# Narrow and wide matmuls take turns on TensorE, gelu as one ScalarE function, zero matmuls and own load tiles at the start, the last token tile in column halves

## The chip, the cores and the metric

The kernel runs on one core of a Trainium2 chip. The metric is the device time of one execution in microseconds (us), as the median of several runs; less is better. The core's engines work side by side, each through its own list of instructions in a fixed order: TensorE (PE, matmuls; PEld is its weight load), VectorE (DVE), ScalarE (ACT), GpSimd (POOL) and SyncE (SP, which here issues nearly all DMA transfers). An instruction that waits holds up everything behind it on its engine.

## The reference, cut to what matters

The program is a decoder trunk of two layers on 512 tokens of width 1024. Every sub-layer is followed by x <- LayerNorm(alpha * x + sublayer(x)).

```python
# layer 0: gated DeltaNet (4 heads, chunks of 64 tokens, a recurrence over chunks)
#          and dilated sliding-window attention (8 heads) from one projection
proj = h @ w_in
dn_qkv, dn_z, dn_b, dn_a, sw_q, sw_k, sw_v = split(proj)
mix = concat([gated_deltanet(...), dilated_attention(...)]) @ w_out
# layer 1: S5, a diagonal complex state space, then gelu and a GLU
y = scan(a_bar, b_bar * u) projected back + d_skip * u
hid = jax.nn.gelu(y)                       # the tanh form
mix = (hid @ w_o) * jax.nn.sigmoid(hid @ w_g)
# both layers, after the mixer
h = post_norm(h, mix)
h = post_norm(h, memory_cross_attention(h, mem, ...))   # 256 memory tokens
h = post_norm(h, (silu(h @ wg) * (h @ wu)) @ wd)         # hidden width 2816
```

## The kernel before, in words

**Products.** A weight block is loaded as fp32 into a tile of the tag `raw` (two buffers), then split: ScalarE copies it rounded to the matmul type fp32r into `hi`, VectorE subtracts, raw - hi, into `lo` (four buffers each). Activations are split in the same way. `mm3` then makes three matmuls of each product, hi·hi, hi·lo and lo·hi. Such a matmul mostly has 512 moving columns (256 in places); these are called wide here. Narrow are the transposes (128x128, against `ident`) and the plain fp32 matmuls of the recurrence and of the attention, most of them 128x128 too. A plain fp32 128x128 matmul that is no transpose stands in the trace as two passes, so the page counts 8220 matmuls where the program has 7618.

**Order.** All work is recorded first, as operations with a priority, and nothing is issued while it is recorded. `Order.order` (line 282 on) then walks through a planned time: whenever an engine is free it takes, from a heap of operations whose inputs are ready in the plan, the one of the best priority whose tiles have a buffer, and books a cost from `Order.cost` (a transpose 0.11 us, a wide matmul of 512 columns 0.217 us, a plain fp32 128x128 matmul 0.217 us in the planner's table). The result is one fixed order for each engine, which `issue` (lines 430 to 439) writes out; hence nearly every row of the trace has line L439, or L437 where several small matmuls go together, and is told apart by the names of its tiles. What the planner believes about a time is not what the chip does: it decides only the order.

**Stages.** Layer 0 begins with `mixer0`: the x tiles and the first weight block of `hyb_w_in` (columns 512 to 768) are loaded at once with a bias of -1000 (lines 615 to 620), through the two `raw` buffers; small constants follow, then the other blocks. A block of 16 small columns of the weights (`t<-in_hyb_w_in_dram`) feeds the gates of the DeltaNet. A solve on VectorE, a chain of narrow matmuls and then a recurrence over chunks follow; wide matmuls of the projections are put between them as far as there are any. Two large constants, `big<-in_ident_dram` (the start value X of the solve) and `big<-in_attmask_dram` (the attention mask), are loaded on SP among the first loads. In layer 1, `s5` goes through eight blocks; each ends in a tile of 128x512 results in PSUM (`yp`), to which gelu is applied by four operations, then four transposes and a split. The GLU, cross-attention and the FFN follow; the FFN's last product (`gemm_tok`, sink `residual_sinks`, `norm_half`) goes token tile by token tile (four of 128 tokens), and the last one ends with VectorE's statistics, the normalisation and the store of the output.

Of the kernel before, what the change touches and what calls it, by code (L numbers as in the profile page):

```python
# [16 lines left out]
P = 128  # L17
# [15 lines left out]
TAIL = 8  # L33
TRIES = 40
FILL = 1
PRE = 1
GATE = 5
STEPS = (4, 2)
LATER = 100
# [65 lines left out]
class Order:  # L105
# [173 lines left out]
    def scratch(self, ap):  # L279
        self.hist.setdefault(ap.tensor.name, ([], []))  # L280


    def order(self, seq, prio):
# [37 lines left out]
        dma_free = 0.0  # L321
        slow = 3.4
        out = []
        for op in ops:
# [3 lines left out]
        while len(out) < n:  # L328
# [5 lines left out]
            for e in self.eng:  # L334
                if busy[e] > now + 1e-9:
                    nxt.append(busy[e])
                    continue
                skipped, got = [], None
                tries = 0
                while heaps[e]:  # L340
# [120 lines left out]
class Trunk:  # L461
# [103 lines left out]

    def gemm_tok_steps(self, w, k0, nk, c0, act, ntt, sink, tail=0):


        pss = [self.bank() for _ in range(ntt)]
        held = []  # L570
        for done in range(0, nk, 2):
            g = min(2, nk - done)
            hi, lo = self.weights(w, k0 + done, g, c0, 512)
            held += [(done + k, hi[:, k], lo[:, k]) for k in range(g)]
            if done + g <= nk - tail:
                self._tok_mms(held, range(ntt), pss, act, nk)
                held = []
                yield
        for tt in range(ntt):
            self._tok_mms(held, [tt], pss, act, nk)  # L580
            sink(tt, pss[tt])
            yield
# [17 lines left out]
    def mixer0(self, fill):  # L600
# [14 lines left out]
        self.o.bias = -1000  # L615
        for kh in range(2):
            view = w_in[kh * 512:kh * 512 + 512, 512:768].rearrange("(k p) c -> p k c", p=P)
            self.early[w_in.tensor.name, kh * 4, 512] = self._load(view, 4, 256, STEPS[kh], lambda s: [
                load_x(kh * 4 + k) for k in range(s * 4 // STEPS[kh], (s + 1) * 4 // STEPS[kh])])
        self.o.bias = 0  # L620
# [221 lines left out]
        def z_sink(tt, ps):  # L842
# [229 lines left out]
    def residual_sinks(self, half, alpha, eps, g, b, last, after):  # L1072

        V, G = self.o.V, self.o.G

        def sink(tt, ps):
            z = self.h[tt][:, half * 512:(half + 1) * 512]
            V.scalar_tensor_tensor(z, z, alpha, ps, op0=OP.mult, op1=OP.add)
            if last:
                self.norm_half(tt, half, eps, g, b, after)  # L1080
        return sink

    def norm_half(self, tt, half, eps, g, b, after):
        V, G = self.o.V, self.o.G
        if half == 0:
            self.stats[tt] = self.tiny(12)
        st = self.stats[tt]
        V.bn_stats(st[:, half * 6:half * 6 + 6], self.h[tt][:, half * 512:(half + 1) * 512])
        if half == 0:
            return  # L1090
        mv = self.tiny(3)
        V.bn_aggr(mv[:, 0:2], st.rearrange("p (n c) -> p n c", n=2))
        V.tensor_scalar(mv[:, 2:3], mv[:, 1:2], eps, None, op0=OP.add)
# [123 lines left out]
    def ffn(self, layer, after, fill=iter(())):  # L1217
# [5 lines left out]
        for part, (b0, b1) in enumerate(FFN_PARTS):  # L1223
# [30 lines left out]
            for half in range(2):  # L1254
                rs = self.residual_sinks(half, 2 * ALPHA if part == 0 else 1.0, 4 * LN_EPS, g, b, last, after)
                self.gemm_tok(wd, b0 * 2, nm, half * 512, htok, NT, rs, tail=TAIL)

# [239 lines left out]
    def s5(self, fill):  # L1497
# [4 lines left out]
        for b in range(8):  # L1502
# [39 lines left out]
            for q in range(4):  # L1542
# [23 lines left out]
    def glu_gate(self, gtok, half):  # L1566
        self.gate = {}

        def sink(tt, ps):
            self.gate[tt] = self.t2()  # L1570
            self.o.A.activation(self.gate[tt], ps, AF.Tanh, scale=0.25)
        return self.gemm_tok_steps(self.a["s5_glu_wg"][0], 0, KT, half * 512, gtok, NT, sink, tail=0 if half == 0 else TAIL)

    def glu(self, gtok):
# [9 lines left out]
        for half in range(2):  # L1584
            def osink(tt, ps):
# [3 lines left out]
                r3 = lambda x: x.rearrange("p (q c) -> p q c", c=32)  # L1589
                V.scalar_tensor_tensor(r3(z), hpv[half][:, tt], 4 * ALPHA, r3(t), op0=OP.mult, op1=OP.add)  # L1590
                self.norm_half(tt, half, 16 * LN_EPS, g, b, after)

# [69 lines left out]
    def setup(self):  # L1662
        nc = self.nc
        self.stats, self.hp, self.early = {}, None, {}
        self.ident = self.const([P, P], name="ident")
# [7 lines left out]
        self.halfpi = self.const([P, 1], name="halfpi")  # L1673
        self.o.V.memset(self.halfpi, math.pi / 2)


# [38 lines left out]
```

## Time and profile before

| | |
|---|---|
| median of 3 runs | 1544.35 us (1540.59 to 1544.91) |
| the profiled execution | 1543.56 us, span 1541.8 us, granted clock 0.995 |
| TensorE busy | 1508.7 us, 98% of the span |
| VectorE, ScalarE, GpSimd busy | 984.9, 552.5, 57.0 us |
| DMA | 184.01 MB, mean 119 GB/s |

The span runs from the first to the last recorded event of the profiled execution; 1.8 us of its time lie outside it. Busy times are sums over the engine's instructions. PE's rows show a duration that includes the pipe (a wide matmul of 0.39 us begins 0.23 us after the one before it), so distances between starts say more than durations.

### The profile page before, as it was taken

Reading aid. Unit: us, or ns where it says so; the run is one execution under the profiler, and the core shown is the slowest. Engines: PE = TensorE matmul, PEld = TensorE weight load, DVE = VectorE, ACT = ScalarE, POOL = GpSimd, SP = SyncE. Lnnn points to the kernel's source line nnn. Section 1 sums busy time; section 2 is a strip of 40 time slices with the busy share of each in tenths; the row PEclk is TensorE's granted clock in tenths of the full one; section 3 lists DMA queues with packets and bytes.
Section 4 is the critical chain, followed back from the end, with each engine's and each line's share of the span. In section 5 each row is a group of like instructions: output and inputs, shape, how many; then the busy total and the mean of one; then the engine's idle time right before and its main releaser. Section 6 shows DMA issues by size and latency. Waiting matters only on the chain.

```text
span 1541.8 us, 21120 instructions
## 1 busy us (share of the span) xinstructions
PE 1508.7 (98%) x8220; PEld 1268.3 (82%) x8220; DVE 984.9 (64%) x1880; ACT 552.5 (36%) x1008; POOL 57.0 (4%) x97
## 2 busy tenths in 40 slices
PE   7999899999999999999999899999999999999998
PEld 5888788689889887888888898888889888888886
DVE  6986576697557888626845899647557444234436
ACT  5533346544523354324341333323423222122311
POOL 1100000010100000010000000000000000000000
PEclk9999999999999999999999999999999999999999
DMA  6424134235223355445562652333212333233322
GB/s 201 115 57 123 47 119 137 64 98 163 62 76 116 110 192 176 150 165 174 186 220 76 245 191 86 128 110 121 65 57 82 109 99 102 85 110 96 96 69 96
DMA packets 125396, 184.01 MB, mean 119 GB/s; under 512 B 14128, under 2 KB 84656, under 8 KB 121200
## 3 DMA queue, kind: packets, MB, share of 16 engines
q1 hardware_dynamic: 125296, 182.66, 37.6%
q8 instruction: 65, 1.06, 0.3%
q14 instruction: 35, 0.29, 0.1%
HBM read 162.45 MB, written 20.19 MB: 118 GB/s over the span
## 4 chain that ended last, share of the span: by engine, by line
PE 88%; DVE 7%; DMA 2%; ACT 1%; issue 1%; SPq 0%; POOL 0%; DVEq 0%; ACTq 0%; POOLq 0%
PE ps L439 86%; DVE t L439 4%; DVE big L439 2%; PE ps L437 2%; DVE lo L439 1%; DMA raw<-in_hyb_w_in_dram 1%; DVE tiny L439 0%; DMA big<-s5m 0%; ACT big L439 0%; DMA raw<-in_xo_w_dram 0%; ACT hi L439 0%; ACT t L439 0%; DMA posi<-in_pos_t_dram 0%; SPq L439 0%; ACT L439 0%
## 5 line engine op out<-in xcount | busy, mean ns | idle before, releaser
L439 PE MATMUL ps<-big,hi 128*128 128x512 f32 (+1 forms) x2368 | 649.5, 360 | 6.1 <-ACT hi L439 4.5
L439 PE MATMUL ps<-hi,big 128*128 128x512 f32 x1728 | 548.2, 394 | 0.7 <-ACT big L439 0.4
L439 PEld LDWEIGHTS ps<-big,hi 128*128 128x128 f32 x2368 | 420.7, 190 | 72.4 <-ACT hi L439 4.7
L439 ACT ACTIVATE hi<-raw 128x1024 fp32r<-128x1024 f32 (+2 forms) x252 | 263.5, 1046 | 513.7 <-PE ps L439 355.7
L439 DVE TENSOR_TENSOR lo<-raw,hi 128x1024 fp32r<-128x1024 f32 (+2 forms) x252 | 303.4, 1205 | 224.8 <-ACT hi L439 221.4
L439 PE MATMUL ps<-big,lo 128*128 128x512 f32 (+1 forms) x1184 | 423.7, 359 | 2.5 <-DVE lo L439 2.5
L439 PEld LDWEIGHTS ps<-hi,big 128*128 128x128 f32 x1728 | 322.6, 188 | 66.4 <-DVE big L439 0.9
L439 PE MATMUL ps<-lo,big 128*128 128x512 f32 x864 | 338.3, 393 | 1.0 <-DVE lo L439 1.0
L439 PEld LDWEIGHTS ps<-big,lo 128*128 128x128 f32 x1184 | 224.6, 190 | 34.5 <-DVE lo L439 2.9
L439 PEld LDWEIGHTS ps<-lo,big 128*128 128x128 f32 x864 | 162.4, 188 | 35.5 <-DVE lo L439 2.2
L439 ACT ACTIVATE big<-ps 128x256 fp32r<-128x256 f32 (+2 forms) x188 | 89.4, 508 | 211.1 <-PE ps L439 202.0
L439 ACT ACTIVATE t<-ps 128x512 f32<-128x512 f32 (+6 forms) x147 | 68.8, 485 | 147.7 <-PE ps L439 139.0
L439 DVE TENSOR_TENSOR big<-ps,big 128x256 fp32r<-128x256 f32 (+1 forms) x152 | 77.6, 541 | 56.9 <-ACT big L439 54.7
L439 DVE SCALAR_TENSOR_TENSOR big<-big,ps 128x512 f32<-128x512 f32 x56 | 38.4, 685 | 86.7 <-PE ps L439 86.7
L439 DVE SCALAR_TENSOR_TENSOR t<-t,ps 128x512 f32<-128x512 f32 x72 | 49.0, 682 | 68.5 <-ACT t L439 49.8
L439 ACT ACTIVATE big<-t 32x128 f32<-32x128 f32 (+2 forms) x148 | 64.9, 455 | 24.3 <-DVE t L439 19.9
L439 DVE SCALAR_TENSOR_TENSOR big<-big,tiny,t 128x512 f32<-128x512 f32 x96 | 66.6, 745 | 0.0
L439 PE MATMUL ps<-ident,t 128*128 128x128 f32 x344 | 62.7, 275 | 3.4 <-ACT t L439 1.8
L439 POOL TENSOR_TENSOR tiny<-tiny,mhalf 128x1 f32<-128x1 f32 (+1 forms) x28 | 23.1, 825 | 962.3 <-DVE tiny L439 953.6
L439 PEld LDWEIGHTS ps<-ident,t 128*128 128x128 f32 x344 | 42.5, 140 | 15.6 <-ACT t L439 5.1
L439 PE MATMUL ps<-big,big 128*128 128x256 f32 (+2 forms) x328 | 54.9, 314 | 0.0
L439 PEld LDWEIGHTS ps<-big,big 128*128 128x128 f32 x328 | 47.8, 190 | 5.0
(145 smaller groups left out, 929.4 us busy)
## 6 DMA issues: line engine op xcount, KB each, us to landing
raw<-in_ffn_wg_dram SPq DMA_DIRECT2D x44, 512.0 KB, 3.8
raw<-in_ffn_wu_dram SPq DMA_DIRECT2D x44, 512.0 KB, 3.6
raw<-in_ffn_wd_dram SPq DMA_DIRECT2D x44, 512.0 KB, 4.1
s5m<-big SPq DMA_DIRECT2D x16, 1024.0 KB, 4.2
big<-s5m SPq DMA_DIRECT2D x16, 1024.0 KB, 6.3
raw<-in_hyb_w_in_dram SPq DMA_DIRECT2D x26, 512.0 KB, 3.8
raw<-in_xk_w_dram SPq DMA_DIRECT2D x16, 512.0 KB, 3.6
raw<-in_xv_w_dram SPq DMA_DIRECT2D x16, 512.0 KB, 4.1
```

The source lines that it names most:

```text
L437: op.inst = getattr(self.eng[e], f)(*a, **k)
L439: op.inst = getattr(self.eng[e], fn)(*args, **kw)
```

## The change

It has six parts. (1) `order` knows two kinds of TensorE operation. After a narrow one it looks, up to 200 entries deep (`WIDE`), for a wide one whose priority is at most 100 (`REACH`) behind the best narrow one, and takes it; and it books 0.08 us less for a narrow operation right after a wide one. (2) gelu is one ScalarE function, `Gelu_apprx_tanh`, in place of Square, a multiply-add on VectorE, Tanh and another; factors of 2 in the GLU are adapted. (3) `setup` puts 14 fp32 matmuls on a tile of zeros ahead of all else. (4) The first weight block goes to a tile of its own instead of the two `raw` buffers, and the second block (columns 768 to 1024) is loaded right behind it. (5) The loads of X and of the attention mask are made to wait for `egl`, a result of the gates, by a one-column copy into their tile. (6) In the second half of the last FFN product the last token tile is computed and normalised in column halves of 256 (60 matmuls of 256 columns in place of 30 of 512), with its statistics in quarters.

```diff
+WARM = 14
+WIDE = 200
+REACH = 100
...
+    def kind(op):
+        _, fn, args, kw, _ = op.alts[0]
+        if fn == "transpose":
+            return "narrow"
+        if fn == "matmul":
+            return "wide" if args[1].dtype == F32R and _size(op.outs[0]) >= 256 else "narrow"
+        return fn
...
+                    if ok and e == "pe" and after == "narrow" and (self.kind(op) != "wide" or narrow is not None and prio[op.i] > prio[narrow.i] + REACH):
+                        narrow = narrow or op
+                        ok = False
...
-                    if tries > TRIES:
+                    if tries > (TRIES if narrow is None else WIDE):
                         break
...
+                got = got or narrow
...
                     if e == "pe":
+                        kind = self.kind(op)
+                        if kind == "narrow" and after == "wide":
+                            cost -= 0.08
+                        after = kind
...
-    def _load(self, view, n, w, steps=1, between=None):
-        raw = self.o.tile(self.wp, [P, 1024], F32, self.nm("raw"), "raw", 2)
+    def _load(self, view, n, w, steps=1, between=None, raw=None):
+        raw = self.o.tile(self.wp, [P, 1024], F32, self.nm("raw"), "raw", 2) if raw is None else raw
...
+            if fine and tt == ntt - 1:
+                for u in range(2):
+                    split_mms(held, [u])
+                    sink(tt, own[u][:, :256], u)
...
+        own = self.big(F32)
+        for cb_ in range(2):
+            for kh in range(2):
+                c0 = 512 + cb_ * 256
...
+                self.early[w_in.tensor.name, kh * 4, c0] = self._load(view, 4, 256, STEPS[kh], lambda s: [
+                    load_x(kh * 4 + k) for k in range(s * 4 // STEPS[kh], (s + 1) * 4 // STEPS[kh])],
+                    own[:, kh * 1024:(kh + 1) * 1024]) if cb_ == 0 else self._load(view, 4, 256)
...
+        V.tensor_copy(X[:, 0, 0:1], egl[:64, 0:1])
         self.o.SP.dma_start(X, a["ident"][0:32, 0:32].partition_broadcast(64))
...
+        V.tensor_copy(attm[:, 0:1], egl[:, 0:1])
         self.o.SP.dma_start(attm, a["attmask"])
...
-            g1, g2 = self.t2(), self.t2()
-            A.activation(g1, yp, AF.Square)
-            V.scalar_tensor_tensor(g1, g1, 1.0 / 0.044715, yp, op0=OP.add, op1=OP.mult)
-            A.activation(g1, g1, AF.Tanh, scale=GELU_C * 0.044715)
-            V.scalar_tensor_tensor(g2, g1, 1.0, yp, op0=OP.add, op1=OP.mult)
+            g2 = self.t2()
+            A.activation(g2, yp, AF.Gelu_apprx_tanh)
...
+        self.o.bias = -3000
+        w, ps = self.t2(), self.bank()
+        self.o.V.memset(w[:, :P], 0.0)
+        for _ in range(WARM):
+            self.o.T.matmul(ps[:, :P], w[:, :P], w[:, :P], start=True, stop=True)
+        self.o.bias = 0
```

Over the whole program a narrow matmul stands directly behind a wide one 241 times before and 449 times after; the wide ones in front of the DeltaNet's chain of narrow matmuls (the one that starts with the transposes `ps<-ident,t` after the solve) number 500 before and 514 after, those inside it, up to the end of the recurrence's narrow run, 44 before and 30 after. ScalarE has 7 table loads after, 5 before. Three places show it.

On TensorE near the start, where the gates' small product (`masks,t`) and the first transposes of x's projections (`ident_72,big`, four to a bank) stand among the wide matmuls of the second weight block (`hi`, `lo`), the order before is:

```order
L439 MATMUL ps_114<-masks,t_39_113 128x8 x4
L439 MATMUL ps_156<-big_77,lo_160 128x512
L439 MATMUL ps_150<-ident_72,big_140 128x128 x4
L439 MATMUL ps_157<-big_77,hi_159 128x512 x2
L439 MATMUL ps_157<-big_77,lo_160 128x512
L439 MATMUL ps_156<-big_78,hi_159 128x512 x2
```

and after the change, at the same place:

```order
L461 MATMUL ps_121<-masks,t_46_120 128x8 x4
L461 MATMUL ps_164<-big_80,hi_97 128x512
L461 MATMUL ps_164<-big_80,lo_98 128x512
L461 MATMUL ps_157<-ident_72,big_147 128x128
L461 MATMUL ps_163<-big_80,hi_97 128x512
L461 MATMUL ps_157<-ident_72,big_147 128x128
L461 MATMUL ps_163<-big_80,hi_97 128x512
L461 MATMUL ps_157<-ident_72,big_147 128x128
L461 MATMUL ps_163<-big_80,lo_98 128x512
L461 MATMUL ps_157<-ident_72,big_147 128x128
L461 MATMUL ps_164<-big_80,hi_97 128x512 x2
```

The four transposes that stood together now have a wide matmul between each two.

On TensorE in the last part of the DeltaNet's chain (`t,big` are plain fp32 matmuls of the recurrence, `ident_72,t` transposes, `hi,big` and `lo,big` wide matmuls of a projection) the order before is:

```order
L439 MATMUL ps_385<-hi_398,big_80 128x512
L439 MATMUL ps_385<-lo_399,big_80 128x512
L439 MATMUL ps_385<-hi_398,big_80 128x512
L439 MATMUL ps_329<-t_252_328,big_97 128x128 x4
L439 MATMUL ps_385<-hi_398,big_80 128x512
L439 MATMUL ps_385<-lo_399,big_80 128x512
L439 MATMUL ps_385<-hi_398,big_80 128x512
L439 MATMUL ps_331<-t_252_328,big_173 128x128 x4
L439 MATMUL ps_339<-t_254_330,big_140 128x128 x4
L439 MATMUL ps_341<-t_264_340,big_195 128x128 x4
```

and after:

```order
L461 MATMUL ps_386<-hi_399,big_82 128x512
L461 MATMUL ps_328<-t_251_327,big_196 128x128 x4
L461 MATMUL ps_334<-t_242_318,big_146 128x128 x4
L461 MATMUL ps_325<-ident_72,t_248_324 128x128 x4
L461 MATMUL ps_330<-t_253_329,big_104 128x128 x4
L461 MATMUL ps_332<-t_253_329,big_174 128x128 x4
L461 MATMUL ps_340<-t_255_331,big_147 128x128 x4
L461 MATMUL ps_342<-t_265_341,big_196 128x128 x4
L461 MATMUL ps_348<-t_255_331,big_146 128x128 x4
L461 MATMUL ps_339<-ident_72,t_262_338 128x128 x4
```

The wide matmuls that stood inside this part are used up ahead of it.

On ScalarE in the first block of S5 (`hi<-raw` splits a weight, `big<-ps` an activation) the order before has Square (`t<-ps`) and Tanh (`t<-t`):

```order
L439 ACTIVATE hi_1520<-raw_1519 128x1024
L439 ACTIVATE t_1385_1462<-ps_1461 128x512
L439 ACTIVATE big_1441<-ps_1490 128x256 x2
L439 ACTIVATE t_1385_1462<-t_1385_1462 128x512
L439 ACTIVATE hi_1542<-raw_1541 128x1024
```

and after the change gelu alone, with a table load ahead of the first one:

```order
L461 ACTIVATE hi_1518<-raw_1517 128x1024
L461 ACT_TABLE_LOAD
L461 ACTIVATE t_1386_1463<-ps_1462 128x512
L461 ACTIVATE t_1422_1499<-ps_1498 128x512
L461 ACTIVATE big_1444<-ps_1464 128x512
```

One ScalarE operation of the block is gone, and with it the two on VectorE that it took turns with.

## Rows read from the trace of the kernel before

**Rows 1.** Page: busy times of the engines, and the chain that ended last.
```profile
PE 1508.7 (98%) x8220; PEld 1268.3 (82%) x8220; DVE 984.9 (64%) x1880; ACT 552.5 (36%) x1008; POOL 57.0 (4%) x97
...
PE 88%; DVE 7%; DMA 2%; ACT 1%; issue 1%; SPq 0%; POOL 0%; DVEq 0%; ACTq 0%; POOLq 0%
```

**Rows 2.** Windows: from:to, length, busy of PE PEld DVE ACT POOL, PEclk, DMA, GB/s.
```profile
28.45:32.60 4.15, 4.15 (x14) 3.28 (x13) 3.95 (x23) 3.51 (x12) 1.19 (x2) 0.59 0.01 4
...
166.00:187.83 21.83, 16.36 (x100) 13.88 (x100) 13.61 (x44) 8.48 (x27) 1.01 (x1) 0.92 0.01 1
...
858.00:873.00 15.00, 10.20 (x81) 9.39 (x80) 13.48 (x19) 4.70 (x7) 0.10 (x1) 0.97 0.65 250
...
875.00:957.00 82.00, 80.64 (x559) 73.22 (x558) 79.68 (x114) 29.29 (x44) 2.54 (x24) 1.00 0.48 157
```

**Rows 3.** Timeline of PE, 4 to 33 us: start, length, instruction, [idle before <-releaser].
```profile
4.53 1.22 PE L439 MATMUL ps<-big,hi 128*128 128x512 f32 x2 [4.53 <-ACT hi L439]
...
8.54 0.69 PE L439 MATMUL ps<-big,hi 128*128 128x512 f32 x2
...
19.13 3.87 PE L439 MATMUL ps<-big,t 128*16 128x512 f32 x16 [1.02 <-DVE t L439]
...
26.78 1.05 PE L439 MATMUL ps<-masks,t 16*128 16x8 f32 x8 [2.42 <-DVE t L439]
...
29.30 1.05 PE L439 MATMUL ps<-big,hi 128*128 128x512 f32 x2
...
32.65 0.40 PE L439 MATMUL ps<-big,lo 128*128 128x512 f32 x1
```

**Rows 4.** Timeline of SP's queue and of ScalarE at the second stall.
```profile
16.79 0.38 SPq L439 DMA_DIRECT2D raw<-in_hyb_w_in_dram  x1
...
22.51 1.06 ACT L439 ACTIVATE hi<-raw 128x1024 fp32r<-128x1024 f32 x1 [4.04 <-DMA raw<-in_hyb_w_in_dram]
...
24.27 1.28 ACT L439 ACT_TABLE_LOAD   x1
25.57 0.31 ACT L439 ACTIVATE sind<-t 128x128 f32<-128x128 f32 x1
```

**Rows 5.** Timeline of PE: transposes alternating, then four together, then wide matmuls alone.
```profile
560.07 0.39 PE L439 MATMUL ps<-big,hi 128*128 128x512 f32 x1
560.30 0.27 PE L439 MATMUL ps<-ident,t 128*128 128x128 f32 x1
560.32 0.48 PE L439 MATMUL ps<-big,hi 128*128 128x512 f32 x1
...
561.67 0.39 PE L439 MATMUL ps<-big,lo 128*128 128x512 f32 x1
...
35.41 0.39 PE L439 MATMUL ps<-big,lo 128*128 128x512 f32 x1
35.64 0.60 PE L439 MATMUL ps<-ident,big 128*128 128x128 f32 x4
...
36.78 0.63 PE L439 MATMUL ps<-big,hi 128*128 128x512 f32 x2
...
1240.26 0.61 PE L439 MATMUL ps<-big,hi 128*128 128x512 f32 x2
...
1240.94 0.61 PE L439 MATMUL ps<-big,hi 128*128 128x512 f32 x2
```

**Rows 6.** Timeline of PE, the longest wait inside the recurrence.
```profile
182.20 5.44 PE L439 MATMUL ps<-t,big 128*128 128x128 f32 x32 [2.34 <-DVE big L439]
```

**Rows 7.** Timeline of VectorE in S5: gelu's first multiply-add and the next instruction.
```profile
881.05 0.69 DVE L439 SCALAR_TENSOR_TENSOR t<-t,ps 128x512 f32<-128x512 f32 x1 [0.61 <-ACT t L439]
881.65 0.69 DVE L439 TENSOR_TENSOR t<-t,t 128x512 f32<-128x512 f32 x1
```

**Rows 8.** Timeline of VectorE behind the last matmul.
```profile
1534.22 0.69 DVE L439 SCALAR_TENSOR_TENSOR big<-big,ps 128x512 f32<-128x512 f32 x1 [0.30 <-PE ps L439]
1534.94 0.69 DVE L439 BATCH_NORM_STATS2 tiny<-big 128x6 f32<-128x512 f32 x1
```

More of the change, by code (lines that the diff above doesn't have):

```diff
@@ L280, in scratch @@
         self.hist.setdefault(ap.tensor.name, ([], []))
+    @staticmethod
+    def kind(op):
[5 more added lines that the diff above has]
+        return fn
     def order(self, seq, prio):
@@ L322, in order @@
         slow = 3.4
+        after = None
         out = []
@@ L337, in order @@
                     continue
-                skipped, got = [], None
+                skipped, got, narrow = [], None, None
                 tries = 0
@@ L564, in gemm_tok, with gemm_tok_steps, split_mms @@
         run(self.gemm_tok_steps(*args, **kw))
-    def gemm_tok_steps(self, w, k0, nk, c0, act, ntt, sink, tail=0):
+    def gemm_tok_steps(self, w, k0, nk, c0, act, ntt, sink, tail=0, fine=False):
         pss = [self.bank() for _ in range(ntt)]
         held = []
+        if fine:
+            own = [pss[ntt - 1], self.bank()]
+        def split_mms(held, us=range(2)):
+            for u in us:
+                cs = slice(u * 256, u * 256 + 256)
+                self._tok_mms([(kt, hi[:, cs], lo[:, cs]) for kt, hi, lo in held], [ntt - 1],
+                              {ntt - 1: own[u][:, :256]}, act, nk)
         for done in range(0, nk, 2):
@@ L575, in gemm_tok_steps @@
             if done + g <= nk - tail:
-                self._tok_mms(held, range(ntt), pss, act, nk)
+                self._tok_mms(held, range(ntt - fine), pss, act, nk)
+                if fine:
+                    split_mms(held)
                 held = []
@@ L579, in gemm_tok_steps @@
         for tt in range(ntt):
-            self._tok_mms(held, [tt], pss, act, nk)
-            sink(tt, pss[tt])
+            if fine and tt == ntt - 1:
+                for u in range(2):
+                    split_mms(held, [u])
+                    sink(tt, own[u][:, :256], u)
+            else:
+                self._tok_mms(held, [tt], pss, act, nk)
+                sink(tt, pss[tt])
             yield
@@ L615, in mixer0 @@
         self.o.bias = -1000
[L616 to L619, printed above, removed]
+        own = self.big(F32)
+        for cb_ in range(2):
+            for kh in range(2):
+                c0 = 512 + cb_ * 256
+                view = w_in[kh * 512:kh * 512 + 512, c0:c0 + 256].rearrange("(k p) c -> p k c", p=P)
+                self.early[w_in.tensor.name, kh * 4, c0] = self._load(view, 4, 256, STEPS[kh], lambda s: [
+                    load_x(kh * 4 + k) for k in range(s * 4 // STEPS[kh], (s + 1) * 4 // STEPS[kh])],
+                    own[:, kh * 1024:(kh + 1) * 1024]) if cb_ == 0 else self._load(view, 4, 256)
         self.o.bias = 0
@@ L1074, in residual_sinks, with sink, norm_half @@
         V, G = self.o.V, self.o.G
-        def sink(tt, ps):
+        def sink(tt, ps, u=None):
             z = self.h[tt][:, half * 512:(half + 1) * 512]
+            if u is not None:
+                z = z[:, u * 256:u * 256 + 256]
             V.scalar_tensor_tensor(z, z, alpha, ps, op0=OP.mult, op1=OP.add)
             if last:
-                self.norm_half(tt, half, eps, g, b, after)
+                self.norm_half(tt, half, eps, g, b, after, u)
         return sink
-    def norm_half(self, tt, half, eps, g, b, after):
+    def norm_half(self, tt, half, eps, g, b, after, u=None):
         V, G = self.o.V, self.o.G
+        quarters = self.fine and tt == NT - 1
         if half == 0:
-            self.stats[tt] = self.tiny(12)
+            self.stats[tt] = self.tiny(24 if quarters else 12)
         st = self.stats[tt]
-        V.bn_stats(st[:, half * 6:half * 6 + 6], self.h[tt][:, half * 512:(half + 1) * 512])
-        if half == 0:
+        if quarters:
+            for i in range(2) if u is None else [u]:
+                n = half * 2 + i
+                V.bn_stats(st[:, n * 6:n * 6 + 6], self.h[tt][:, n * 256:(n + 1) * 256])
+        else:
+            V.bn_stats(st[:, half * 6:half * 6 + 6], self.h[tt][:, half * 512:(half + 1) * 512])
+        if half == 0 or u == 0:
             return
         mv = self.tiny(3)
-        V.bn_aggr(mv[:, 0:2], st.rearrange("p (n c) -> p n c", n=2))
+        V.bn_aggr(mv[:, 0:2], st.rearrange("p (n c) -> p n c", c=6))
         V.tensor_scalar(mv[:, 2:3], mv[:, 1:2], eps, None, op0=OP.add)
@@ L1255, in ffn @@
                 rs = self.residual_sinks(half, 2 * ALPHA if part == 0 else 1.0, 4 * LN_EPS, g, b, last, after)
-                self.gemm_tok(wd, b0 * 2, nm, half * 512, htok, NT, rs, tail=TAIL)
+                self.fine = layer == 1 and last
+                self.gemm_tok(wd, b0 * 2, nm, half * 512, htok, NT, rs, tail=TAIL, fine=self.fine and half == 1)
     def to_out(self):
@@ L1570, in sink @@
             self.gate[tt] = self.t2()
-            self.o.A.activation(self.gate[tt], ps, AF.Tanh, scale=0.25)
+            self.o.A.activation(self.gate[tt], ps, AF.Tanh, scale=0.5)
         return self.gemm_tok_steps(self.a["s5_glu_wg"][0], 0, KT, half * 512, gtok, NT, sink, tail=0 if half == 0 else TAIL)
@@ L1589, in osink @@
                 r3 = lambda x: x.rearrange("p (q c) -> p q c", c=32)
-                V.scalar_tensor_tensor(r3(z), hpv[half][:, tt], 4 * ALPHA, r3(t), op0=OP.mult, op1=OP.add)
-                self.norm_half(tt, half, 16 * LN_EPS, g, b, after)
+                V.scalar_tensor_tensor(r3(z), hpv[half][:, tt], 2 * ALPHA, r3(t), op0=OP.mult, op1=OP.add)
+                self.norm_half(tt, half, 4 * LN_EPS, g, b, after)
             if half:
@@ L1663, in setup @@
         nc = self.nc
-        self.stats, self.hp, self.early = {}, None, {}
+        self.stats, self.hp, self.early, self.fine = {}, None, {}, False
         self.ident = self.const([P, P], name="ident")
```

## The prediction

> **What bounds the kernel now.** I read the page's busy times and its chain first, then the windows by stage, then TensorE's timeline where a window showed idle time, then the timelines of the engines that it waited for. TensorE is busy 98% of the span and has 88% of the chain that ended last; VectorE has 7% of the chain and no other engine more than 2% [rows 1]. So time can go away in two ways only: TensorE does its matmuls faster, or one of its waits goes. The span is 1541.8 us and PE's busy time 1508.7, so all waits together are 33 us, some 4.5 of them before the first matmul and 7.6 from VectorE's last multiply-add on behind the last (1541.8 - 1534.22) [rows 8]. The waits inside stand in few places: 1.02 and 2.42 us at the start [rows 3]; 21.83 - 16.36 = 5.5 us in the recurrence, the longest of them 2.34 [rows 2, 6]; 4.8 us at the beginning of S5 (858 to 873) and 1.4 over the next 82 us, in which VectorE is as busy as TensorE, 79.7 against 80.6 us [rows 2].
>
> **Part 1, taking turns.** This is the largest part by count: 208 more narrow matmuls stand directly behind a wide one (449 - 241), and the planner books 0.08 us less for each, 16.6 us in all. The trace has both patterns. Three wide matmuls alone go from start 1240.26 to 1240.94: 0.227 each [rows 5]. From 560.07 to 561.67 stand five wide and four transposes in turns: (1.60 - 5 x 0.227) / 4 = 0.116 for each transpose [rows 5]. From 35.41 to 36.78 stand four wide and four transposes, the four together: (1.37 - 4 x 0.227) / 4 = 0.116 again [rows 5]. The 0.03 us after which the wide matmul begins behind a transpose is what looks like a gift; the matmul after it begins 0.32 later in place of 0.23. So turns save nothing on TensorE: I take 0. Its bounds are -16.6 (all that the planner books) and +2.1, an estimate: a hundredth of a microsecond each, which is the rounding of the two values. The Trainium skill, "TensorE: Matmul & The Clock Gate", Part 2, step 1, says that the engine pulls a weight load ahead of running matmuls, so that the next tile's weights come in while this one runs. That speaks for turns (a narrow matmul's load would lie under the wide one); by it the term could be a gain, which the rows above do not show.
>
> What turns do change is the order. 14 wide matmuls move from inside the DeltaNet's chain to the stretch ahead of it (500 to 514 before it, 44 to 30 in it). Inside the chain TensorE waits for VectorE and ScalarE, and a wide matmul there fills a wait. 14 x 0.227 = 3.2 us of cover are gone; what is late is the chain itself, which was 5.5 us short of work already. The matmuls' own time is the same wherever they stand, so the loss is between 0 (the chain starts 3.2 us earlier than it would have, if its inputs are there) and 3.2; I take half, +1.6, since the solve on VectorE gives the chain its start and I can't see how much of that wait the plan shifts.
>
> **Parts 3, 4 and 5, the start.** Zeros: 14 fp32 matmuls are 28 passes. The first product waits until 4.53 for ScalarE's split, and TensorE has nothing to do until then [rows 3]. From 4.53 to 8.54 nine wide matmuls begin 0.446 apart, against 0.227 later: the lower of the two clocks, 1.2 in place of 2.4 GHz, by the spacing (the stretch from 28.45 to 32.60 has the same spacing and a granted clock of 0.59 in its row) [rows 2, 3]. If the engine is already fast when the first product comes, 9 x 0.22 = 2.0 us are gained. But the zeros run at the lower clock too: a pass at about 0.2 us (twice 0.116 less a little, an estimate) makes 28 x 0.2 = 5.6 us, so begun at some 0.7 they end at about 6.3, and the products that stand behind them start 1.8 us late. As products queued up behind the zeros then run at 0.227, I take -0.8; bounds +2.4 (late and no faster) and -1.9.
>
> Own tile and early load: in the trace the second block's second half is issued on SP at 16.79, since a `raw` buffer comes free only then and the large constants X and mask stand ahead; ScalarE's split of it waits 4.04 us for that transfer, to 22.51, and holds the table load (24.27) and the sine (25.57) behind it, on which VectorE and so TensorE's wait of 2.42 at 26.78 rest [rows 3, 4]. After, that block is issued right behind the first loads, and nothing but the split of the x tiles stands before it. I take both stalls as gone: -3.4. With them goes what they cause: after the 2.42 us gap the matmuls from 29.30 to 32.65 run at the lower clock, eight starts in 3.35 us in place of 8 x 0.227 = 1.82: -1.5 [rows 2, 3]. What is late next is the small block of 16 columns, which is still behind the constants on SP; if it stalls TensorE in their place, 0 to 2.4 us come back. X and the mask wait for `egl`, which comes after the gates; the solve needs X only much later, and nothing else waits on SP behind them that TensorE needs. I cost that at 0; if the cover were gone, a stall like the 2.42 us one.
>
> The start is -0.8 - 3.4 - 1.5 = -5.7, and with the loss in the chain -4.1. This is the bulk of the forecast.
>
> **Part 2, gelu.** Each of eight blocks loses two VectorE operations of 0.69 us, behind which the next instruction begins 0.60 later: 16 x 0.60 = 9.6 us of VectorE's time [rows 7], and one of ScalarE's two. But the time only counts where TensorE waits for it: 1.4 us from 875 to 957 [rows 2], and I add 0.6 for the blocks behind that, an estimate from the same window. The first comes at 881.05 [rows 7], so the 4.8 us before 873 are not gelu's; a shorter VectorE queue might let the planner rearrange them. I take -2.5: the 2.0 and half a microsecond of these. Bounds 0 and -8 (1.4 + 0.6 + 4.8 and what of the low clock goes with it).
>
> The price is two more table loads, one before the first gelu and one before cross-attention's exponentials. In the trace a load takes 1.28 us and the next ScalarE instruction begins directly behind it, 24.27 + 1.28 = 25.55 against 25.57 [rows 4]. ScalarE is busy 29.3 of the 82 us [rows 2], which hides both: 0, and +2.6 if both lie on the path. The Trainium skill, "ScalarE: Activation LUTs", What ACT_TABLE_LOAD costs, puts a switch at 1.28 us and another 1.38 for a drain; by it the bound would be +5.3 in place of +2.6. The rows show the first, and no drain.
>
> **Part 6, the tail.** Behind the last matmul come a multiply-add and statistics of 0.69 us each on 512 columns [rows 8]. In halves, the last piece has 256 columns; between half of 0.69 and all of it I take 0.42 for each, an estimate near the half, so 2 x 0.27 = -0.54. Against it 60 matmuls of 256 columns for 30 of 512 cost the same by columns; I allow +0.4 for their number. Sum -0.15, which is nothing here, bounds -0.7 and +0.4.
>
> **Sum.** -0.8 - 3.4 - 1.5 + 1.6 - 2.5 - 0.15 = -6.75, made against the profiled execution: 1543.56 - 6.75 = 1536.8, and its time is 0.8 us under the median of 1544.35. I say 1537.
>
> **The rivals.** *Slower (chance 0.13).* The planner credits TensorE with 208 x 0.08 = 16.6 us that rows 5 do not show. The lists of the other engines are therefore made for a TensorE that is ahead of the real one; an instruction of VectorE that waits for a late matmul holds up ones behind it that TensorE needs next. Where TensorE is the bound, this is harmless, since a late planned instruction finds others already done. In S5 and the recurrence, where VectorE is as busy as it, each microsecond of error can become a wait. If all of it does, -6.75 + 16.6 = +10, 1553.5; it decides from about 7 us of it on, where the gain is eaten. Against it speaks that most of the 16.6 us lie in places where PE's row has no idle time.
> *Turns do pay (0.10).* If the records' starts mislead, and a narrow matmul's load is hidden in turns, then up to 16.6 us more go: 1520; with 0.057 in place of 0.116 for each, half a slot, 12 us: 1525. The rows at 560 us speak against it plainly.
> *The change doesn't do what it says: no difference (0.17).* The solve and the chain start from VectorE's results, not from TensorE's, so 5.7 us won at the start are waited out before the recurrence; S5 stays bound by VectorE's scans and gains its 2 us at most. Then -0.5 to -2: about 1542.5. For it speaks that every wide matmul ahead of the chain is a fixed amount of work only as long as TensorE, not VectorE, ends last there.
> The forecast itself has 0.60.
>
> **How the numbers follow.** The smallest difference that can be told here is about 0.3%, 4.6 us, so faster means under 1539.7. The forecast's own range is 1530 to 1541 (S5's bound of -8 below; start stalls that come back, the chain's 3.2 and a table load above); five sixths of it, 0.50, are faster, the rest, 0.10, within 0.3%. With the turns' 0.10, faster is 0.60; with 0.17, the same is 0.27; slower 0.13. The range for 8 in 10 reaches from the turns' weaker form at 1525 to 1547, and leaves out the stronger form and most of the slower rival.
>
> **What would show it.** Right: the waits of 1.02 and 2.42 us and the granted clock of 0.59 behind them are gone; PE's first product starts nearer to 6 than to 4.5, with starts 0.23 apart; in turns, a wide and a narrow matmul together still take 0.34; the recurrence has more idle time than 5.5 us; VectorE has some 10 us less between 860 and 978, and PE's idle time there falls by 2 to 3; two new table loads sit in ScalarE's idle time; the tail is half a microsecond shorter. Wrong: pairs in turns that take 0.28, or idle time on PE in stages that had none (cross-attention, the FFN), or a chain that starts no earlier than before.

## The result, and the profile after

The changed kernel takes 1556.01 us (1555.35 to 1556.36, 4 runs) against 1543.17 us of before (4 runs): ratio 1.0084, 95% interval 1.0067 to 1.0102. It is 13 us slower, outside the stated range of 1525 to 1547, where 1537, some 7 us faster, was forecast. The page, in the places that answer to [rows 1]:

```profile
span 1554.0 us, 21231 instructions
...
PE 1519.0 (98%) x8278; PEld 1273.5 (82%) x8278; DVE 973.1 (63%) x1870; ACT 552.5 (36%) x1002; POOL 60.2 (4%) x97
...
PE 91%; DVE 6%; ACT 2%; issue 1%; DMA 0%; POOL 0%; DVEq 0%; ACTq 0%; POOLq 0%
```

PE is as busy in share as before, but its busy time grew by 10.3 us (1519.0 - 1508.7); the zeros' row below is 5.4 of them. VectorE lost 11.8 us of work, as gelu's edit should have it, and the span grew all the same.

**The start** came out in the rows much as forecast. PE's timeline, answering to [rows 3]:

```profile
1.05 5.43 PE L461 MATMUL ps<-t 128*128 128x128 f32 x28 [1.05 <-DVE t L461]
6.24 0.70 PE L461 MATMUL ps<-big,hi 128*128 128x512 f32 x2
6.78 0.40 PE L461 MATMUL ps<-big,lo 128*128 128x512 f32 x1
7.01 0.62 PE L461 MATMUL ps<-big,hi 128*128 128x512 f32 x2
...
8.40 0.62 PE L461 MATMUL ps<-big,hi 128*128 128x512 f32 x2
...
26.29 0.27 PE L461 MATMUL ps<-ident,big 128*128 128x128 f32 x1
26.32 0.48 PE L461 MATMUL ps<-big,hi 128*128 128x512 f32 x1
26.64 0.27 PE L461 MATMUL ps<-ident,big 128*128 128x128 f32 x1
...
31.94 0.30 PE L461 MATMUL ps<-ident,big 128*128 128x128 f32 x1 [0.93 <-DVE tiny L461]
```

The first product begins at 6.24, behind the zeros, and the first nine wide matmuls take 2.16 us (to 8.40), where before they took 4.01 (4.53 to 8.54). So what the zeros gain on these nine they lose by starting later: the tenth wide matmul begins 0.14 us earlier than before. The waits of 1.02 and 2.42 us are gone, with the slow stretch behind them; one of 0.93 is new. The rows at 26.29 to 26.64 are turns: a narrow and a wide matmul together take 0.35 us, as they did at 560 us before [rows 5]. By step 1 of the Trainium skill's "TensorE: Matmul & The Clock Gate", Part 2, the narrow one's weights could have come in under the wide one; whatever is overlapped there, the pair has not become shorter.

**The loss** shows first in the recurrence. The windows of after, answering to [rows 2]:

```profile
160.00:170.00 10.00, 7.80 (x54) 6.54 (x52) 3.01 (x13) 4.71 (x14) 1.01 (x1) 0.96 0.01 2
170.00:180.00 10.00, 6.61 (x26) 5.76 (x27) 3.96 (x14) 1.88 (x9) 0.00 (x0) 0.50 0.00 0
180.00:190.00 10.00, 7.67 (x41) 7.46 (x41) 6.50 (x21) 3.76 (x8) 1.01 (x1) 0.69 0.01 2
```

TensorE's granted clock is 0.50 from 170 to 180: its lower level, 1.2 GHz, for the whole window, and 0.69 in the next. PE's timeline tells why. The view ends at 190 us and so cuts its last row: the group that begins at 185.96 has 32 passes and takes 5.44 us, as it did before [rows 6].

```profile
165.72 1.06 PE L461 MATMUL ps<-t,big 128*128 128x128 f32 x8
167.69 1.02 PE L461 MATMUL ps<-ident,t 128*128 128x128 f32 x4 [0.91 <-DVE t L461]
171.05 2.04 PE L461 MATMUL ps<-t,big 128*128 128x128 f32 x8 [2.33 <-DVE big L461]
174.31 2.08 PE L461 MATMUL ps<-t,big 128*128 128x128 f32 x8 [1.22 <-DVE t L461]
177.07 2.07 PE L461 MATMUL ps<-t,big 128*128 128x128 f32 x8 [0.69 <-ACT t L461]
179.59 3.60 PE L461 MATMUL ps<-t,big 128*128 128x128 f32 x16 [0.44 <-DVE t L461]
183.02 0.60 PE L461 MATMUL ps<-ident,t 128*128 128x128 f32 x4
185.96 4.21 PE L461 MATMUL ps<-t,big 128*128 128x128 f32 x21 [2.33 <-DVE big L461]
```

Nothing but narrow matmuls and waits stand here. Behind the waits of 0.91 and 2.33 us the clock falls, and from then on eight passes take 2.04 to 2.08 us, where eight took 1.06 at 165.72. The same groups in the kernel before:

```profile
168.93 0.40 PE L439 MATMUL ps<-hi,big 128*128 128x512 f32 x1
170.10 1.13 PE L439 MATMUL ps<-t,big 128*128 128x128 f32 x8 [0.77 <-DVE big L439]
...
172.44 1.16 PE L439 MATMUL ps<-t,big 128*128 128x128 f32 x8 [0.52 <-DVE t L439]
174.29 1.16 PE L439 MATMUL ps<-t,big 128*128 128x128 f32 x8 [0.69 <-ACT t L439]
175.89 2.23 PE L439 MATMUL ps<-t,big 128*128 128x128 f32 x16 [0.44 <-DVE t L439]
178.84 1.02 PE L439 MATMUL ps<-ident,t 128*128 128x128 f32 x4 [0.72 <-DVE t L439]
```

There wide matmuls stood ahead of the first group and behind it (the rows left out after 170.10 are three of them). From 172.44 on the groups were bare too, but the clock had not fallen by then. The four groups of 8, 8, 8 and 16 passes took 5.68 us in all (1.13 + 1.16 + 1.16 + 2.23), and now take 9.79 (2.04 + 2.08 + 2.07 + 3.60): 4.1 us more. The waits of the stretch, with the one of 2.3 us at its end, were 5.5 us and are now 7.9: 2.4 more.

Where the statistics of the first token tile that end mixer 0 are aggregated on VectorE, the changed kernel is 6.7 us late (326.33 against 319.65); at the end of the first cross-attention 9.1 (488.13 against 479.03), through S5 10, at the end 12.2 (1547.82 against 1535.67).

**S5** shows the edit working and paying nothing. The window that stands to the changed kernel's later time as 875 to 957 did before:

```profile
885.00:967.00 82.00, 80.86 (x561) 73.68 (x561) 69.08 (x97) 28.66 (x41) 2.21 (x22) 0.99 0.44 145
```

VectorE is busy 69.1 us, 10.6 less; TensorE's idle time is 1.14 against 1.36 us.

**The tail** became worse. VectorE's timeline, answering to [rows 8]; PE's last matmul begins at 1545.26:

```profile
1540.25 0.68 DVE L461 SCALAR_TENSOR_TENSOR big<-big,ps 128x512 f32<-128x512 f32 x1
1542.70 0.42 DVE L461 SCALAR_TENSOR_TENSOR big<-big,ps 128x256 f32<-128x256 f32 x1 [1.76 <-PE ps L461]
1543.04 1.01 DVE L461 BATCH_NORM_STATS2 tiny<-big 128x6 f32<-128x512 f32 x2
1543.97 0.19 DVE L461 BATCH_NORM_AGGREGATE tiny<-tiny 128x2 f32<-128x12 f32 x1
1544.19 0.15 DVE L461 TENSOR_SCALAR tiny<-tiny 128x1 f32<-128x1 f32 x1
1544.26 2.73 DVE L461 SCALAR_TENSOR_TENSOR big<-big,tiny,t 128x512 f32<-128x512 f32 x4
1546.91 0.41 DVE L461 SCALAR_TENSOR_TENSOR big<-big,ps 128x256 f32<-128x256 f32 x1
```

The multiply-add of the last tile's first half (1542.70) stands ahead of the third tile's statistics and waits 1.76 us for its matmuls. The third tile's normalisation is late by that, and so the second half's multiply-add begins at 1546.91, 1.65 us after the last matmul began; before it was 0.43 (1534.22 - 1533.79).

### The profile page after: what moved, and what is told of

Same layout as the page of the kernel before. It is cut to its first block, busy times and chain, and to the rows that moved or that the text cites. A ratio compares the mean times of both kernels' runs of the same rounds, so it can differ in the third digit from the quotient of the medians.

```text
span 1554.0 us, 21231 instructions
## 1 busy us (share of the span) xinstructions
PE 1519.0 (98%) x8278; PEld 1273.5 (82%) x8278; DVE 973.1 (63%) x1870; ACT 552.5 (36%) x1002; POOL 60.2 (4%) x97
## 3 DMA queue, kind: packets, MB, share of 16 engines
q8 instruction: 65, 1.06, 0.3%
## 4 chain that ended last, share of the span: by engine, by line
PE 91%; DVE 6%; ACT 2%; issue 1%; DMA 0%; POOL 0%; DVEq 0%; ACTq 0%; POOLq 0%
PE ps L461 89%; DVE big L461 2%; PE ps L459 2%; DVE t L461 2%; DVE lo L461 1%; ACT big L461 1%; DVE tiny L461 1%; ACT t L461 0%; ACT L461 0%; DMA raw<-in_xq_w_dram 0%; ACT hi L461 0%; POOL tiny L461 0%; DVEq L1766 0%; ACT sind L461 0%; DVE cin L461 0%
## 5 line engine op out<-in xcount | busy, mean ns | idle before, releaser
L461 PE MATMUL ps<-hi,big 128*128 128x512 f32 (+1 forms) x1748 | 556.1, 395 | 0.0
L461 DVE TENSOR_TENSOR lo<-raw,hi 128x1024 fp32r<-128x1024 f32 x246 | 300.0, 1222 | 228.1 <-ACT hi L461 226.2
L461 ACT ACTIVATE hi<-raw 128x1024 fp32r<-128x1024 f32 x246 | 260.3, 1059 | 511.6 <-PE ps L461 348.6
L461 PEld LDWEIGHTS ps<-hi,big 128*128 128x128 f32 x1748 | 325.9, 188 | 65.9 <-issue 0.3
L461 PE MATMUL ps<-lo,big 128*128 128x512 f32 (+1 forms) x874 | 344.3, 395 | 0.5 <-DVE lo L461 0.5
L461 DVE SCALAR_TENSOR_TENSOR big<-big,ps 128x512 f32<-128x512 f32 (+1 forms) x57 | 38.3, 672 | 85.5 <-PE ps L461 85.4
L461 PE MATMUL ps<-ident,t 128*128 128x128 f32 x344 | 75.6, 276 | 5.9 <-ACT t L461 4.2
L461 DVE SCALAR_TENSOR_TENSOR t<-t,ps 128x512 f32<-128x512 f32 x56 | 38.2, 683 | 57.2 <-ACT t L461 40.6
L461 PEld LDWEIGHTS ps<-ident,t 128*128 128x128 f32 x344 | 44.9, 141 | 17.3 <-ACT t L461 6.4
L461 PE MATMUL ps<-t,big 128*128 128x128 f32 (+1 forms) x288 | 46.9, 299 | 7.9 <-DVE big L461 5.5
```

What stands on the lines that cost most here:

```text
L461: op.inst = getattr(self.eng[e], fn)(*args, **kw)
```

## The experiments

Theory A: the planner's turns use up the wide matmuls that covered the recurrence's waits, and TensorE's clock falls there. Theory B: turns cost time on TensorE wherever they happen. Theory C: another part costs. All ratios are to the kernel before, run on the same chip. Unless said otherwise an edit is to the changed kernel.

**e1 to e4: the two halves of part 1.** e1 leaves out both the search and the booking, e2 the booking alone, e3 the search alone; e4 is the kernel before with part 1 alone.

```diff
e1, e3
-                    if ok and e == "pe" and after == "narrow" and (self.kind(op) != "wide" or ...
+                    if False and ok and e == "pe" and after == "narrow" and (self.kind(op) != "wide" or ...
e1, e2
-                        if kind == "narrow" and after == "wide":
+                        if False and kind == "narrow" and after == "wide":
                             cost -= 0.08
```

> The changed kernel without part 1 (neither the search for a wide matmul nor the 0.08 us booked off), all else kept. In the order 494 wide matmuls stand ahead of the chain and 28 come back in the recurrence's last third. Theory A (the planner's turns use up the wide matmuls that covered the recurrence's waits, and TensorE falls to its lower clock there): the recurrence's stretch with a granted clock of 0.5 goes, 12 to 17 us faster than the changed kernel, about 1540. Theory B (taking turns itself costs TensorE time wherever it happens): also about 1540, but the gain is spread over the span, not in 160 to 200 us. Theory C (another part costs: gelu's table loads, the tail, the late X and mask): 1553 to 1556.

> The changed kernel with the search for a wide matmul after a narrow one, but without the 0.08 us that the planner books off; 495 narrow matmuls stand right behind a wide one, more than in the changed kernel (449), but the wide matmuls in front of and inside the recurrence stand as in the kernel without turns (494 ahead, 28 in the last third). Theory A: within 3 us of the kernel without turns, about 1541. Theory B: no better than the changed kernel, 1554 to 1558. Theory C: 1553 to 1556.

> The changed kernel with the 0.08 us booked off where a narrow matmul happens to stand behind a wide one, but without the search; 253 such pairs. 500 wide matmuls ahead of the chain, 13 in the last third of the recurrence in place of 28. Theory A: between the two, 1542 to 1548. Theory B: as the kernel without turns, about 1540. Theory C: 1553 to 1556.

> The kernel before with part 1 alone (search and 0.08 us). 514 wide matmuls ahead of the chain, 19 in the recurrence's last stretch that had 28. Theory A: the recurrence loses its cover, 5 to 10 us slower than before, 1549 to 1554. Theory B: 10 us or more slower, spread over the span. Theory C: within 2 us of before, 1543.

| | wide matmuls ahead of the chain | median us | ratio, interval |
|---|---|---|---|
| e1, neither | 494 | 1541.24 | 0.9991 (0.9982 to 1.0000) |
| e2, search alone | 494 | 1543.23 | 1.0002 (0.9992 to 1.0013) |
| e3, booking alone | 500 | 1546.00 | 1.0027 (1.0016 to 1.0038) |
| changed, both | 514 | 1556.01 | 1.0084 (1.0067 to 1.0102) |
| e4, both, nothing else | 514 | 1562.16 | 1.0134 (1.0117 to 1.0150) |

e2 has more pairs in turns (495) than the changed kernel (449) and all of its other parts, and none of its loss of 13 us: B and C fall as its cause. The booking is what costs, 5.6 us without the search (1.0027 against 0.9991) and 12.7 with it (1.0084 against 1.0002). e4 was 20.7 us slower, far beyond what theory A had for it (theory B's "10 us or more" would take it in, but e2 speaks against B); nothing else is in it, so the other parts of the change gave some 8 us back. About 4 of them are in S5: between the statistics ahead of it and behind it e4 falls back from +13.2 to +17.3 us against the kernel before, the changed kernel from +9.9 to +10.2. Gelu's shorter list on VectorE may pay there, against a loss that part 1 brings; no run has part 1 with gelu alone, so this is not shown. In e1 the recurrence's windows have no clock of 0.5:

```profile
160.00:170.00 10.00, 9.21 (x57) 7.72 (x56) 4.87 (x18) 2.37 (x8) 1.01 (x1) 1.00 0.00 0
170.00:180.00 10.00, 6.50 (x45) 5.37 (x44) 5.90 (x21) 3.51 (x12) 1.01 (x1) 1.00 0.00 0
180.00:190.00 10.00, 10.00 (x65) 9.32 (x65) 7.87 (x27) 5.91 (x17) 1.37 (x1) 0.83 0.50 180
```

**e5, e8: work added to the recurrence.** The same four matmuls are done again, into a bank that nobody reads, behind `kS` and `vp` of each step. e8 does it without parts 1 and 6.

```diff
+        def again(mm):
+            spare = self.bank()
+            for h in range(4):
+                mm(spare[:, hsl(h)], h)
...
+                again(lambda x, h: T.matmul(x, sk[:, h, ts], St[:, hsl(h)], start=True, stop=True))
...
+            again(lambda x, h: T.matmul(x, TT[:, hsl(h)], r[:, hsl(h)], start=True, stop=True))
```

> The changed kernel with more work: behind the first and the second product of each recurrence step the same four matmuls again, into a spare bank that nobody reads (7 groups of 4, 56 passes, 6 us at the upper clock). The wide matmuls stand as in the changed kernel. If a good part of the loss in the recurrence is TensorE's lower clock there (theory A in full), the granted clock of 0.5 from 170 to 187 us goes and the kernel is 2 to 6 us faster although it does more, 1550 to 1554. If only the missing cover counts, and the clock does not, it is the same or up to 6 us slower, 1556 to 1562.

> Without parts 1 and 6, with the repeated matmuls in the recurrence. Where the wide matmuls already cover part of the waits, the added 6 us find less room: theory A says that the rest of the low clock (0.83 in 180 to 190 us) goes and some wide matmuls move behind the chain, in sum within 3 us of the same kernel without the added work, 1538 to 1542. If added work counts in full: 1545.

e5: 1554.90, ratio 1.0077 (1.0062 to 1.0092), by its interval not to be told from the changed kernel's 1.0084, with 56 passes more. Its windows:

```profile
160.00:170.00 10.00, 10.00 (x81) 9.46 (x79) 2.83 (x12) 4.04 (x13) 1.01 (x1) 1.00 0.00 0
170.00:180.00 10.00, 7.80 (x50) 7.25 (x49) 5.42 (x20) 3.14 (x12) 1.01 (x1) 0.83 0.01 2
180.00:190.00 10.00, 8.11 (x69) 7.87 (x69) 8.28 (x28) 5.42 (x16) 0.58 (x1) 1.00 0.40 144
```

The window of 170 to 180 us has 0.83 in place of 0.50. The time lies between the two expectations and decides for neither. The trace says more: from the transposes ahead of the bare groups to the first wide matmul behind them e5 takes 21.6 us (168.31 to 189.94), the changed kernel 23.5 (167.69 to 191.15), though e5 does more in it. So the clock, back for most of the stretch, paid for the added work there: that the low clock is part of the price is shown; that it is all of it is not. e8: 1541.70, 0.9988 (0.9978 to 0.9997), against 0.9976 of e6 below: 2 us dearer, as theory A had it.

**e6, e7: without the halves.** e6 is e1 without part 6, e7 is e2 without it.

```diff
-                self.fine = layer == 1 and last
+                self.fine = False
```

> The changed kernel without part 1 and without part 6 (no column halves, no quarters): start and gelu alone. If the halves cost 1.2 us (VectorE's list has the half's multiply-add ahead of the third tile's statistics), it is 1.0 to 1.5 us faster than the changed kernel without part 1, about 1540, and 3 to 4 under before. If the halves cost nothing, the same as that kernel.

> The changed kernel without the 0.08 us and without part 6, with the search for a wide matmul kept. Theory A: 1.0 to 1.5 us faster than the same with halves, about 1541.5. If the search itself is a gain in mixer 0 (its end came 4 us earlier than without it), a kernel without the later loss in cross-attention would show it; here no more than 1 us to the kernel without turns is expected.

e6: 1539.17, 0.9976 (0.9967 to 0.9985); e7: 1540.18, 0.9983 (0.9973 to 0.9992). Both are 2 to 3 us under their twins with halves (0.9991, 1.0002). In the profiles, the last aggregation stood in e1 1.3 us worse against the kernel before than the first tile's of the same stage (-2.81 against -4.14 us), in e6 not (-3.23 both). The other 1 us lies within the intervals. The search alone costs about 1 us (e7 against e6), within the intervals.

**e9: half the booking.**

```diff
-                            cost -= 0.08
+                            cost -= 0.04
```

> The changed kernel with 0.04 us booked off in place of 0.08. In the order the wide matmuls in front of and in the recurrence stand as in the changed kernel (514 ahead, 8 in the last third), though the planner's error per pair is half. If what counts is where the wide matmuls end up (theory A), the time is that of the changed kernel in the recurrence, 1552 to 1557 in all. If each microsecond of the planner's error costs by itself (the slower rival of the prediction as it was put), it lies half way between the 1543.2 without booking and 1556.0: 1549.6.

1555.19, 1.0079 (1.0064 to 1.0094): the changed kernel's time at half the error. What counts is where the wide matmuls end up.

**e13, e14: the booking up to and from planned time 190 us.**

```diff
-                        if kind == "narrow" and after == "wide":
+                        if kind == "narrow" and after == "wide" and now < 190:     # e14: now >= 190
```

> The changed kernel with 0.08 us booked off only up to planned time 190 us; the order up to the end of the recurrence is that of the changed kernel. If all of the booking's 12.8 us comes from the recurrence's lost cover, directly or behind it: 1554 to 1557. If the recurrence's part is what the rows there show, 9 to 10 us above the kernel without booking (1543.2): 1552 to 1553.

> The changed kernel with 0.08 us booked off only from planned time 190 us on; the order up to the end of the recurrence is that of the kernel with the search and no booking. If all comes from the recurrence: 1543, no different from the kernel without booking. If the later stages have an error of their own: 1545.5 to 1547.

e13: 1550.45, 1.0049 (1.0031 to 1.0067); e14: 1546.59, 1.0025 (1.0015 to 1.0034). Over e2 that is 7.3 and 3.6 us (0.0047 and 0.0023 of 1543), 10.9 of the booking's 12.7; the rest lies within the intervals. By the medians the recurrence costs less than the 9 to 10 us that its rows suggested, but the rows come from single executions: e13's profiled one is the slowest of its four (1552.44), e2's the fastest of its ten (1541.17), 11.3 us apart, and of these 10.7 stand at the end of the bare groups (191.93 against 181.26).

How the 7.3 come about can be read from the same stretch as above. In e2 it takes 20.65 us (160.61 to 181.26) and has 20 wide matmuls in it; in the changed kernel 23.46 us (167.69 to 191.15) with none. The narrow matmuls are the same. So 4.5 us of wide matmuls (20 x 0.227) are done ahead of the stretch, and the stretch, with that much less in it, takes 2.8 us longer: 7.3 in all.

The later stages have a loss of their own. e14's profiled execution is 6.0 us longer than e2's (1547.21 against 1541.17), and 5.0 of them stand at the first statistics that end mixer 0 (317.99 against 312.98). The loss shows between 280 and 300 us, with a clock of 0.83; e2's row for the same window, shown second, has 1.00:

```profile
280.00:300.00 20.00, 18.29 (x126) 12.75 (x127) 10.11 (x31) 11.71 (x25) 0.00 (x0) 0.83 0.18 55
...
280.00:300.00 20.00, 19.62 (x146) 14.84 (x143) 11.91 (x32) 10.70 (x22) 0.00 (x0) 1.00 0.38 120
```

**e10 to e12: the other parts alone.** The kernel before with the hunks of part 2 (e10), of parts 3 to 5 (e11), and of parts 4 and 5 (e12).

> The kernel before with part 2 alone. By the prediction's term -2.5 us (0 to -8), 1540.5. By the changed kernel without turns, where the end of S5 stood no more than 0.2 us better than its beginning and the next stage 1 us: 0 to -1.3, 1542 to 1543.

> The kernel before with parts 3, 4 and 5 (zeros, own tiles and early load, X and mask behind the gates). By the prediction's start term -5.7 us, 1537.3. By the end of mixer 0 in the changed kernel without turns, -2.8: 1540 to 1541.

> As e11, without the 14 zero matmuls. The prediction gave the zeros 0.8 us of the start's gain. If they are worth that or less, this kernel is 0 to 1 us slower than e11; if the low clock over the first nine wide matmuls (2 us) and later ones comes back, 2 us or more.

e10: 1543.56, 0.9996 (0.9984 to 1.0008; one of its ten runs, at 4189.61 us, is left out of the ratio). e11: 1538.63, 0.9971 (0.9962 to 0.9981), under both the kernel before and the changed one, and with e6 the fastest of the study (the two can't be told apart). e12: 1541.17, 0.9986 (0.9977 to 0.9995). So gelu is worth nothing that can be told, the start 4.5 us, and the zeros with what they change in the order some 2.3 of them. (Across S5 e10's profile gains 1.2 us on that of the kernel before; those of e11 and e12, which have gelu in four operations as before, gain 1.2 and 1.1.) Of the PE timelines the rows at which zeros could matter, e12's first, then e11's:

```profile
4.41 1.22 PE L442 MATMUL ps<-big,hi 128*128 128x512 f32 x2 [4.41 <-ACT hi L442]
...
18.61 3.87 PE L442 MATMUL ps<-big,t 128*16 128x512 f32 x16 [0.97 <-DVE t L442]
...
7.05 0.81 PE L442 MATMUL ps<-big,hi 128*128 128x512 f32 x2
...
19.94 3.88 PE L442 MATMUL ps<-big,t 128*16 128x512 f32 x16
```

Without zeros the first products begin at 4.41, and the wait before the small product is there again (0.97 us, 1.02 before); with them, in e11, it is not. But the start itself is no earlier by them: e11's nine first wide matmuls take 2.24 us in place of 3.76, they begin 2.64 us later, and the small product comes at 19.94 in place of 18.61. What e11 has is another order. The planner has placed six wide matmuls more inside the DeltaNet's chain (494 ahead of it and 50 in it, e12 500 and 44), the waits in the chain are 4.3 us in place of 5.6, and at its end e11 is 0.5 us ahead (185.30 against 185.84). That the 2.3 us come from this order and not from the clock at the start is likely but not shown: no run has the zeros with e12's order, and single executions of one order differ by more than 0.5 us.

## Why the prediction was wrong, point by point

- **The step that failed** is the cover: "14 wide matmuls move from inside the DeltaNet's chain to the stretch ahead of it", with a loss between 0 and 3.2 us, of which I took +1.6. I priced the moved matmuls by their own duration, and the chain's clock at nothing. What they did was to keep TensorE working between the recurrence's narrow groups. Without them the waits are bare and the clock falls. The waits grew by 2.4 us, which the bound allowed; the 40 passes of the four groups took 9.79 us in place of 5.68, and these 4.1 us alone are more than the bound that I had set on the whole. Measured, the booking up to the end of the recurrence costs 7.3 us (e13 against e2). I had the low clock at the start in the same profile (0.59 behind a wait of 2.42 us) and did not apply it to the chain.
- **A second place** was not seen: the booking from planned time 190 us on costs 3.6 us more (e14), most of it in mixer 0's later part, where the clock is lower again (0.83 against 1.00). I looked only at the recurrence's rows.
- **Turns on TensorE, 0:** right. 0.35 us for a pair after as before; the search alone costs 1 to 2 us, by intervals that overlap. The bound of +2.1 held.
- **The slower rival** (the planner's credit of 16.6 us makes the lists wrong) named the culprit, at a chance of 0.13, but not the mechanism: I had each microsecond of error turn into a wait of another engine. Half the error costs the same (e9), and the loss follows the wide matmuls that the plan spends ahead of the chain: 514 with either booking, 494 without. Why a booking makes the planner move them was not taken apart.
- **The start, -5.7:** near in size, -4.5 (e11), but by two errors that nearly cancel. Without the zeros it measured -2.2 (e12) where I had -4.9: of the stalls of 1.02 and 2.42 us, 0.97 before the small product stayed in e12, and a new one of 1.57 came at 32.31 (0.93 at 31.94 in the changed kernel). The zeros were taken at -0.8 and are worth about -2.3 (e11 against e12), beyond my bound of -1.9 if only just, and not by my mechanism: what the fast first products won, the later start took back, and the gain appears only behind the start, where the order differs. That my sum for the start came close is luck.
- **Gelu, -2.5:** mis-sized; it measured 0 (e10, interval -2.5 to +1.2 us). VectorE did lose 10.6 us in the window, and TensorE's idle time there fell by 0.2. My bound of 0 was the answer: the 10.6 us were time for which TensorE hardly waited. The two table loads are in e10's sum, and it shows no cost that can be told. One of them does stand in a wait: it begins at 889.51 in the changed kernel, when TensorE's result is there, takes 1.28 us, and the first gelu begins at 890.81, directly behind it. The Trainium skill ("ScalarE: Activation LUTs", What ACT_TABLE_LOAD costs) has 2.66 us for a switch, with a drain of 1.38; these rows show none behind the load.
- **The tail, -0.15:** wrong sign, +1.3 by e1's profile, about 2 us by the ratios of e1 and e6. I counted the halves' durations and did not ask what is queued behind the first half's multiply-add on VectorE.

## What to carry to other kernels

Filler matmuls in a chain that waits on other engines can be worth more than their duration (here 20 of them, 4.5 us, were worth 7.3): count what the chain's own matmuls cost when TensorE falls to its lower clock. In a planner with a cost table, check a new discount against the distance between starts of a whole pair, and look in the order for what is used up earlier because of it. Splitting a last tile pays only if nothing that is due sooner stands behind the first half's wait. And a part that is tried alone in a planned kernel changes the order too: compare the orders before a gain is put down to the part.

## What had not been expected of the hardware

Adding 56 matmul passes, about 6 us at the upper clock, to a chain in which TensorE waits left the time as it was (1.0077 against 1.0084), with the granted clock of 170 to 180 us at 0.83 in place of 0.50. In the stretch itself the added work even ended sooner (21.6 us in place of 23.5).
